# Tensors of the first stage stored by chunk, queries kept on chip, and new assumed durations in a planned two-layer decoder kernel

## The chip, the cores and the metric

The kernel runs on one core of one Trainium2 chip. The metric is the device time of one execution in microseconds (us), the median of three runs. The core has five engines with instruction streams of their own: TensorE (PE, matmuls and transposes), VectorE (DVE), ScalarE (ACT), GpSimd (POOL) and SyncE (SP), and DMA queues that are fed by SP, ACT and POOL.

## The reference

Two layers of a decoder for 2048 prompt tokens and 8 sample tokens, width 1024, fp32. Cut to what matters:

```
layer 0 (even):  p = rmsnorm(x) @ w_in -> val, gate, gate_a, q, k, v, z, beta, a
   A: c = conv31(val * sigmoid(gate)); silu(layernorm(c)) * silu(gate_a)
   B: q, k, v = silu(conv4(q, k, v)); gated delta rule over the tokens, 4 heads of 128:
        per chunk: u, w from a triangular solve of k, v, beta, decay
        v_new = u - w @ S;  o = q @ S + (q k^T * decay) @ v_new;  S = g * S + k^T @ v_new
      rmsnorm(o) * silu(z)
   x += concat(A, B) @ w_out
   x += cross_attention(rmsnorm(x), memory)           # 4 heads of 256, 256 memory rows
layer 1 (odd):   causal mean pooling over 2/4/8/16 tokens, a map per group, gate, w_out; then attention
y = rmsnorm(x);  also new conv, delta, pool states and memory keys and values
```

The sample tokens take the same path one step at a time, with cached memory keys and values of their own (8 x 256 rows for each layer).

## The kernel before

All activations lie transposed: channels on partitions, tokens on columns. A dense product is made of three fp32r matmuls (high x high, low x high, high x low), so each weight tile `rraw` is split into `rhi` and `rlo`, and each activation into a pair (`hh`/`hl`, `mh`/`ml`, `xh`/`xl`).

The stages: memory keys and values (`kv`, with the first norms beside it); the input projection in blocks of columns (gate, val, qkv, z) over five token tiles of 512, 512, 512, 260 and 260 columns, with the 31-tap convolution on DVE (`cacc`, 240 instructions over 1024 tokens each) and the 4-tap one (`qacc`); the delta rule over 16 chunks of 128 tokens, with matrices of the memory attention (`G`, `VW`, weights by memory) as dense filling; output projection; attention 0; the odd layer; attention 1 and the last norm. Beside these run the sample tokens' steps as side work.

The program has no hand-written order. A planner (class `Flow`, here `F`) writes it: every call (`F.mm`, `F.act`, `F.stt`, `F.dma` and so on) issues one instruction and moves an assumed clock of its engine by an assumed duration, and remembers at what assumed time each tile is written. Stages of dense matmuls are generators; after each piece `F.pump()` looks through the side tasks and runs one step of each whose inputs are ready by the assumed clock of PE. So the assumed durations set where the side work stands between the dense matmuls, and with that the order on every engine. `F.move`, `F.rows` and `F.ve` also choose ACT, DVE or POOL by these clocks. A DMA whose source isn't ready by the assumed clock is held back (`F.pend`) and issued later. The result is one fixed list of instructions for each engine; at run time each engine goes through its list in order and waits on semaphores.

Two assumed durations are touched. A matmul in fp32r of n columns costs `max(n, 248) * 0.422` ns. A DMA is assumed to start 650 ns after its issue, to move 360 bytes for each ns on one ring, and to be seen 900 ns later:

```
        x = max(g + 650, self.ring)
        self.ring = x + nb / 360.0
        self.mark(ri, ro, "dma", self.ring, self.ring + 900)
```

The assumed costs of DVE, ACT and POOL are not touched; that of a `cacc` (1024 columns by `F.stt`) is 1024/0.96 + 130 ns.

In the input projection, `fin_z` and the task after the 4-tap convolution store z and q, k, v to DRAM, `d_z` and `d_qkv`, in tiles `so` of 128 x 512, by head: `[4 or 12, 128, tokens]`. A bank `ps_mm` of a val block is free once DVE has written `glu` from it.

In the delta rule `prep(n)` loads k and q of a chunk, makes `qk` and `A`; later steps invert `A` by blocks (`ad`, `lo`, `UT`, `b`, `x`), `scan` walks the chunks with the state `S`, and a last task norms `o`, multiplies it with z and stores `d_b`. Q is loaded twice: by `prep` into `q` (three places), and by `scan` into `q2` (two places), two chunks ahead. In `scan`, PE runs `ps_bg<-S,k` and `ps_bg<-S,q2`, DVE makes `x`, PE `ps_bg<-x,A`, ACT or DVE `vn`, PE `ps_bg<-vn,kd` and `ps_bg<-vn,qk`, and DVE the new `S`.

Norms sum squares with a matmul of ones (`ps_ss`, from `acc` or `w_sqa`) and spread the result over partitions with a diagonal: DVE writes `dg` or `w_sqq<-ident,rr`, PE `ps_bc` (function `spread`; `tok_spread` calls it for the later stages). The sample's cross attention (`sample_attn`) loads cached keys and values through POOL's queue, 256 KB each, into three buffers `a_big`, with `d_sq` (the query spread out) or `d_sp` (the probabilities) in one of them for two loads of the cache, and DVE multiplies the two and sums: 128 products `a_big<-a_big` of 128 x 256 for each layer.

Of the kernel before, what the change touches and what calls it, by code (L numbers as in the profile page):

```python
# [55 lines left out]
class Flow:  # L56
# [106 lines left out]
    def mm(self, out, lhsT, rhs, start=True, stop=True, cost=None):  # L163
        n = fsz(rhs)
        if cost is None:
            cost = max(n, 248) * 0.422 if lhsT.dtype == F32R else max(n, 64) * 1.69
        self.pe_op(cost, out, lhsT, rhs)
        self.nc.tensor.matmul(out, lhsT, rhs, start=start, stop=stop)  # L168
# [123 lines left out]
    def _dma(self, out, in_, eng, t):  # L292
        ri, ro = [self.region(in_)], [self.region(out)]
        if eng == "sync" and out.space == DRAM and self.hand.get(in_.tensor.name) == {"act"}:
            eng = "scalar"
        s = max(self.t[eng], t, self.ready(ri, ro, eng))
        nb = 4
        for _, c in out.ap:
            nb *= c
        if eng == "scalar":  # L300
            s = max(s, self.t["act"])
            self.t["act"] = self.t[eng] = g = s + 360
        elif eng == "gpsimd":
            s = max(s, self.t["pool"])
            self.t["pool"] = self.t[eng] = g = s + 1060
        else:
            self.t[eng] = s + 50
            s = max(s, self.hw)
            self.hw = g = s + 475
        x = max(g + 650, self.ring)  # L310
        self.ring = x + nb / 360.0
        self.mark(ri, ro, "dma", self.ring, self.ring + 900)
        getattr(self.nc, eng).dma_start(out=out, in_=in_)
# [123 lines left out]
def spread(F, C, pool, ppool, r, n, tag, dg=None):  # L437

    ncn = (n + 127) // 128
    if dg is None:  # L440
        dg = pool.tile([128, ncn * 128], F32, tag=tag + "dg", name="dg")
    for c in range(ncn):
        F.ts(dg[:, c * 128:(c + 1) * 128], C.ident, r[:, c:c + 1], ALU.mult)
    yield
    ps = ppool.tile([128, 512], F32, tag="bg", name="ps_bc")
    F.mm(ps[:, 0:n], C.ones, dg[:, 0:n])
    return ps


def ceil128(n):  # L450
    return (n + 127) // 128 * 128
# [200 lines left out]
def phase1(F, C, I, D, st, P, R, mmp, bgp, loaders, mix, hp):  # L652
# [38 lines left out]
    with F.tile_pool(name="x1", bufs=1, side="right") as xp:  # L691
# [77 lines left out]
        def fin_z(b, t, n, ps):  # L769
            o = DT[t][0]  # L770
            z = sop.tile([128, 512], F32, tag="so", name="so", bufs=2)
            F.act(z[:, 0:n], ps[:, 0:n], AF.Silu)
            F.dma(D.z[b][:, o:o + n], z[:, 0:n])

# [147 lines left out]
    def conv4(b, t):  # L922
        yield qfree.ok
        qfree.take()
        r = rawt[b, t]
        acc = bp.tile([128, 512], F32, tag="qacc", name="qacc", bufs=2)
        F.copy(acc, r[:, 0:512], scale=C.scw[:, b, 0:1])
        for i in range(1, 4):
            F.stt(acc, r[:, i:i + 512], C.scw[:, b, i:i + 1], acc, ALU.mult, ALU.add)
        rfree.give()  # L930
        yield
        z = sop.tile([128, 512], F32, tag="so", name="so", bufs=2)
        F.act(z, acc, AF.Silu)
        F.dma(D.qkv[b][:, t * 512:(t + 1) * 512], z)
        qfree.give()
        qdone.add((b, t))
# [120 lines left out]
def phase2(F, C, I, D, st, P, fill, hp, mmp, bgp, after):  # L1057
# [15 lines left out]
    def small(tag, first, n, shape=(128, 4, 128)):  # L1073

        i = left[tag] = left.get(tag, -1) + 1
        return hp.tile(list(shape), F32, tag=f"h{first + i % n}", name=tag, bufs=1)

    hu = {}

    def room(tag, n):  # L1080

        q, b = (dx, 2) if n % 8 in (4, 5) else (cq, SL - 2)
        if tag == "A":
            return q.tile([128, 2, 4, 128], F32, tag=tag, name=tag, bufs=b // 2)
        return q.tile([128, 4, 128], F32, tag=tag, name=tag, bufs=b)
# [8 lines left out]
    gate = {n: getattr(st, n).rearrange("p (h c) -> p h c", h=4) for n in ("gc", "egc", "ekd", "gl")}  # L1094
    qkv = D.qkv.rearrange("(x h) p t -> x p h t", x=3)
    zv = D.z.rearrange("h p t -> p h t")

# [5 lines left out]
    def prep(n):  # L1103
        yield lambda: nxt[0] == n and cq and (n < 4 or dx) and slots.n >= 2 - n % 2 and (n < SL or n // 2 - (SL+1)//2 in done["T"])
        nxt[0] += 1
# [4 lines left out]
        X.A = X.A2[:, n % 2]  # L1110
        tok = slice(128 * n, 128 * n + 128)
        X.k = room("k", n)
        dec = small("dec", 0, NP)
        q = small("q", NP, NP)
        F.dma(X.k, qkv[1][:, :, tok])
        F.dma(q, qkv[0][:, :, tok])
        yield
# [37 lines left out]
        v = small("v", 2 * NP, 3)  # L1155
        F.dma(v, qkv[2][:, :, tok])
        F.now()
        ad = small("ad", 2 * NP + 3, NP, (128, 4, 48))
        a16 = ad[:, :, 32:48]
# [129 lines left out]

    def load_q(n):  # L1290
        q = big("q2", 2)
        F.dma(q, qkv[0][:, :, 128 * n:128 * n + 128])
        return q

    def scan():
        yield lambda: sq
        S = [sq.tile([128, 128], F32, name=f"S{h}") for h in range(4)]
        for h in range(4):
            F.memset(S[h], 0.0)
        qn = [load_q(0), load_q(1)]  # L1300
        for n in range(16):
            yield lambda: n in done["L"]
            X, q = hu[n], qn.pop(0)
            pk, pq = ps4(), ps4()
# [25 lines left out]
            F.tt(o, po, qs, ALU.add)  # L1330
            if n + 2 < 16:
                qn.append(load_q(n + 2))
                F.now()
            yield
# [7 lines left out]
    def onorms(i):  # L1342
        for n in range(i, 16, 2):
            yield lambda: n in oq
            o, ss = oq.pop(n)
            z = sq.tile([128, 4, 128], F32, tag=f"z{i}", name="z", bufs=1)
            F.dma(z, zv[:, :, 128 * n:128 * n + 128])
            F.now()
# [16 lines left out]
            F.stt(z, pt, C.dng[:, 0:1], z, ALU.mult, ALU.mult)  # L1365
            F.dma(D.b[n // 2].rearrange("h p t -> p h t")[:, :, 128 * (n % 2):128 * (n % 2) + 128], z)
            ofree.give()
# [118 lines left out]
def tok_spread(F, C, W, r, n):  # L1486
    return spread(F, C, W.p, W.bgp, r, n, "w", dg=W.t("sqq", [128, ceil128(n)]))

# [14 lines left out]
def e2(F, C, W, I, D, st, R, bdone, over, grow, spawn):  # L1503
# [33 lines left out]
    def prep():  # L1537
        for g in range(NG):
# [7 lines left out]
            b = W.t("f", [128, 4, n])  # L1546
            F.dma(b, D.b[g].rearrange("b p t -> p b t"))
            tb = F.cur
# [523 lines left out]
def sample_mix(F, C, p, bgp, I, D, st):  # L2072
# [144 lines left out]
    yield lambda: "z" in st.done  # L2217
    F.dma(zs, D.z.rearrange("h p t -> p h t")[:, :, SEQ:NT])
    F.tt(kd, o, o, ALU.mult)
# [5 lines left out]
    F.stt(o, o, C.dng[:, 0:1], zs.rearrange("p a b -> p (a b)"), ALU.mult, ALU.mult)  # L2225
    F.dma(D.b[0].rearrange("h p t -> p h t")[:, :, 256:264], o.rearrange("p (a b) -> p a b", a=4))
    yield lambda: free.n == 3
# [415 lines left out]
```

## Time and profile before

| | |
|---|---|
| median of three runs | 2902.09 us (2898.34 to 2905.38) |
| the profiled execution, its own time | 2902.86 us |
| its span | 2901.1 us |
| mean granted clock of PE | 0.972 |
| busy: PE / DVE / ACT / POOL | 2730.5 / 1968.4 / 1032.0 / 657.0 us |
| moved by DMA | 377.85 MB, 130 GB/s over the span |

The times are those of whole executions; the profile is one of them, and its span runs from the first to the last instruction that it shows. A row of a group names the line of the kernel, the engine, the operation, the tile written and the tiles read. Nearly all instructions are issued by helpers, so lines are those of helpers (L168 `mm`, L172 `tr`, L186 `act`, L219 `tt`, L225 `stt`, L232 `ts`, L313 a DMA) and the tiles tell what it is. A wait names the engine that stood, what it was about to do, and what it waited for last.

### The profile page before, as it was taken

To read this page: it belongs to the slowest core of one execution; us is meant where nothing else is said; L and a number is where in the kernel's file an instruction comes from. 1 tells how busy PE (TensorE), PEld (TensorE's weight loads), DVE (VectorE), ACT (ScalarE), POOL (GpSimd) and SP (SyncE) were. 2 spreads that over 40 slices of the span, in tenths; PEclk is the share of its full clock that TensorE was granted. 3 is DMA by queue.
4 is the path that set the end of the run, shared out by engine and by line. 5 is a ranking of instruction groups with operands and counts; after the bars stand their busy time and mean duration, and the time that the engine had idled before them with its cause. 6 is when DMAs were issued, how large, how long until landed. Compare 5 with 4: busy or idle time off the path is not lost.

```text
span 2901.1 us, 52440 instructions
## 1 busy us (share of the span) xinstructions
PE 2730.5 (94%) x20202; PEld 2498.5 (86%) x20202; DVE 1968.4 (68%) x4612; ACT 1032.0 (36%) x2448; POOL 657.0 (23%) x936
## 2 busy tenths in 40 slices
PE   7999999999998889799999999899999998999997
PEld 6878888888888778699898889899999997789987
DVE  6838999988667887776655556867755445765453
ACT  5632232233356455432321325443422122432321
POOL 3301112111054355122232320111011111221210
PEclk9999999999989899899999999999999999999998
DMA  7611122123455557565645434322545556422211
GB/s 240 213 48 41 46 75 65 46 77 113 129 148 160 154 165 230 172 228 183 211 149 169 144 117 140 116 70 74 173 134 165 181 165 206 136 78 68 70 59 52
DMA packets 269194, 377.85 MB, mean 130 GB/s; under 512 B 46096, under 2 KB 168208, under 8 KB 268944
## 3 DMA queue, kind: packets, MB, share of 16 engines
q1 hardware_dynamic: 211776, 264.77, 29.4%
q0 software_dynamic: 20864, 67.39, 7.5%
q10 hardware_dynamic: 36304, 42.34, 4.2%
q8 instruction: 159, 2.61, 0.4%
q14 instruction: 91, 0.75, 0.1%
HBM read 276.38 MB, written 96.40 MB: 128 GB/s over the span
## 4 chain that ended last, share of the span: by engine, by line
PE 34%; DMA 9%; DVE 6%; issue 2%; ACT 1%; POOL 1%; DVEq 0%; SPq 0%; POOLq 0%; ACTq 0%
PE ps_mm L168 32%; DMA a_big<-d_sp 2%; DVE a_big L225 1%; DMA a_big<-d_sq 1%; DMA a_big<-in_cache_v 1%; PE ps_pt L172 1%; DMA w_f<-d_x 1%; DVE rlo L225 1%; DVE w_d L219 1%; DMA rraw<-d_VW 1%; PE ps_row L168 1%; DVE rlo L219 1%; DVE ml L219 0%; DMA rraw<-d_G 0%; DMA a_big<-in_cache_k 0%
## 5 line engine op out<-in xcount | busy, mean ns | idle before, releaser
L219 POOL TENSOR_TENSOR rlo<-rraw,rhi 128x512 fp32r<-128x512 f32 x143 | 209.1, 1470 | 579.0 <-ACT rhi L186 495.5
L225 DVE SCALAR_TENSOR_TENSOR cacc<-glu,dww,cacc 128x1024 f32<-128x1024 f32 x240 | 325.6, 1369 | 5.9 <-ACT cacc L186 1.4
L219 POOL TENSOR_TENSOR w_sqb<-w_sqb,w_sqq 128x512 f32<-128x512 f32 (+1 forms) x101 | 137.1, 1357 | 660.9 <-ACT w_sqq L186 653.9
L168 PE MATMUL ps_mm<-xh,rhi 128*128 128x256 f32 (+1 forms) x1920 | 274.0, 285 | 5.3 <-DVE pool_sm L219 3.2
L168 PE MATMUL ps_mm<-xl,rhi 128*128 128x256 f32 (+1 forms) x1920 | 273.1, 284 | 0.0
L168 PE MATMUL ps_mm<-xh,rlo 128*128 128x256 f32 (+1 forms) x1920 | 272.7, 283 | 0.0
L168 PEld LDWEIGHTS ps_mm<-xh,rhi 128*128 128x128 f32 x1920 | 250.6, 192 | 8.6 <-issue 3.4
L168 PEld LDWEIGHTS ps_mm<-xl,rhi 128*128 128x128 f32 x1920 | 250.0, 192 | 2.6
L168 PEld LDWEIGHTS ps_mm<-xh,rlo 128*128 128x128 f32 x1920 | 248.2, 191 | 1.0
L168 PE MATMUL ps_mm<-hh,rhi 128*128 128x512 f32 (+2 forms) x1152 | 216.8, 329 | 20.2 <-ACT hh L186 15.8
L219 DVE TENSOR_TENSOR w_y<-ps_mm,w_y 128x256 f32<-128x256 f32 (+1 forms) x248 | 103.4, 420 | 165.6 <-PE ps_mm L168 161.2
L168 PE MATMUL ps_mm<-hh,rlo 128*128 128x512 f32 (+2 forms) x1152 | 214.6, 328 | 0.0
L168 PEld LDWEIGHTS ps_mm<-hh,rhi 128*128 128x128 f32 x1152 | 177.9, 191 | 42.0 <-ACT hh L186 16.2
L168 PE MATMUL ps_mm<-hl,rhi 128*128 128x512 f32 (+2 forms) x1152 | 211.7, 326 | 0.0
L225 DVE SCALAR_TENSOR_TENSOR a_big<-a_big 128x256 f32<-128x256 f32 x256 | 105.0, 448 | 144.5 <-DMA a_big<-d_sp 78.3
L186 ACT ACTIVATE rhi<-rraw 128x512 fp32r<-128x512 f32 x235 | 143.8, 628 | 164.0 <-DMA rraw<-d_G 41.5
L168 PEld LDWEIGHTS ps_mm<-hh,rlo 128*128 128x128 f32 x1152 | 175.9, 191 | 19.4 <-issue 2.2
L168 PEld LDWEIGHTS ps_mm<-hl,rhi 128*128 128x128 f32 x1152 | 175.4, 190 | 17.3
L168 PE MATMUL ps_mm<-mh,rhi 128*128 128x256 f32 (+1 forms) x1152 | 170.1, 288 | 11.8 <-ACT mh L186 11.7
L168 PE MATMUL ps_mm<-ml,rhi 128*128 128x256 f32 (+1 forms) x1152 | 170.5, 290 | 2.5 <-DVE ml L219 2.5
L168 PEld LDWEIGHTS ps_mm<-mh,rhi 128*128 128x128 f32 x1152 | 153.6, 195 | 14.5 <-ACT mh L186 12.8
L168 PE MATMUL ps_mm<-mh,rlo 128*128 128x256 f32 (+1 forms) x1152 | 165.6, 284 | 0.0
(425 smaller groups left out, 5344.5 us busy)
## 6 DMA issues: line engine op xcount, KB each, us to landing
w_f<-d_x SPq DMA_DIRECT2D x60, 512.0 KB
d_x<-w_y SPq DMA_DIRECT2D x44, 512.0 KB
w_y<-d_x SPq DMA_DIRECT2D x44, 512.0 KB
a_big<-in_cache_k POOLq DMA_DIRECT2D x64, 256.0 KB, 4.0
a_big<-in_cache_v POOLq DMA_DIRECT2D x64, 256.0 KB, 4.1
rraw<-in_w_in SPq DMA_DIRECT2D x56, 256.0 KB
d_qkv<-so ACTq DMA_DIRECT2D x48, 256.0 KB
rraw<-in_w_xk SPq DMA_DIRECT2D x32, 256.0 KB
```

The lines of the kernel that those rows point to most:

```text
L168: self.nc.tensor.matmul(out, lhsT, rhs, start=start, stop=stop)
L172: self.nc.tensor.transpose(out, in_, ident)
L186: self.nc.scalar.activation(out=out, in_=in_, func=func, scale=scale, **kw)
L219: self._e(eng).tensor_tensor(out=out, in0=a, in1=b, op=op)
L225: self._e(eng).scalar_tensor_tensor(out=out, in0=a, scalar=s, in1=b, op0=op0, op1=op1, **kw)
```

## The change

Three things are changed.

1. Assumed durations: an fp32r matmul of n columns now costs `max(n, 240) * 0.426 + 9` ns (512 columns: 227 for 216; 256: 118 for 108); a DMA starts 925 ns after its issue, moves 270 bytes for each ns, and is seen 1000 ns later.
2. Layouts: `d_qkv`, `d_z` and `d_b` are laid out by chunk, 128 partitions by 4 heads by 128 tokens, so that a load of a chunk takes 2 KB in one piece from each partition, and a store of 128 x 512 is written in pieces of 512 bytes. z of the sample tokens goes to a tensor of its own, and a tile of z that ends inside a chunk is stored in two pieces.
3. `q` of `prep` stays on chip until `scan` has read it, in one of eight places (`qplace`); `load_q` and its 16 loads go. `prep` waits, for two of eight chunks, until the pool `sq` of these places is open. `ad` has two buffers for three. And `spread` looks up the bank's pool after its yield instead of at the call.

```diff
-            cost = max(n, 248) * 0.422 if lhsT.dtype == F32R else max(n, 64) * 1.69
+            cost = max(n, 240) * 0.426 + 9 if lhsT.dtype == F32R else max(n, 64) * 1.69
...
-        x = max(g + 650, self.ring)
-        self.ring = x + nb / 360.0
-        self.mark(ri, ro, "dma", self.ring, self.ring + 900)
+        x = max(g + 925, self.ring)
+        self.ring = x + nb / 270.0
+        self.mark(ri, ro, "dma", self.ring, self.ring + 1000)
...
-    ps = ppool.tile([128, 512], F32, tag="bg", name="ps_bc")
+    ps = getattr(ppool, "bgp", ppool).tile([128, 512], F32, tag="bg", name="ps_bc")
...
-            F.dma(D.z[b][:, o:o + n], z[:, 0:n])
+            a = o
+            while a < min(o + n, SEQ):
...
+            if o + n > SEQ:
+                F.dma(D.zs[:, b, :], z[:, SEQ - o:NT - o])
...
-        F.dma(D.qkv[b][:, t * 512:(t + 1) * 512], z)
+        F.dma(D.qkv[b // 4, 4 * t:4 * t + 4, :, b % 4, :].rearrange("c p t -> p c t"), z.rearrange("p (c t) -> p c t", c=4))
...
+    def qplace(n):
+        i = n % 8
+        if i < 6:
+            return hp.tile([128, 4, 128], F32, tag=f"h{(NP, NP + 1, NP + 2, 11, 12, 13)[i]}", name="q", bufs=1)
+        return sq.tile([128, 4, 128], F32, tag="q", name="q", bufs=2)
...
-        yield lambda: nxt[0] == n and cq and (n < 4 or dx) and slots.n >= 2 - n % 2 and (n < SL or n // 2 - (SL+1)//2 in done["T"])
+        yield lambda: nxt[0] == n and cq and (n < 4 or dx) and (n % 8 < 6 or sq) and slots.n >= 2 - n % 2 and (n < SL or n // 2 - (SL+1)//2 in done["T"])
...
-        q = small("q", NP, NP)
-        F.dma(X.k, qkv[1][:, :, tok])
-        F.dma(q, qkv[0][:, :, tok])
+        q = X.q = qplace(n)
+        F.dma(X.k, D.qkv[1, n])
+        F.dma(q, D.qkv[0, n])
...
-        ad = small("ad", 2 * NP + 3, NP, (128, 4, 48))
+        ad = small("ad", 2 * NP + 3, 2, (128, 4, 48))
...
-    def load_q(n):
-        q = big("q2", 2)
-        F.dma(q, qkv[0][:, :, 128 * n:128 * n + 128])
-        return q
...
-            X, q = hu[n], qn.pop(0)
+            X = hu[n]
+            q = X.q
...
-            if n + 2 < 16:
-                qn.append(load_q(n + 2))
-                F.now()
...
-            F.dma(z, zv[:, :, 128 * n:128 * n + 128])
+            F.dma(z, D.z[n])
...
-        D.qkv = dr.tile([12, 128, SEQ], F32, name="d_qkv")
-        D.z = dr.tile([4, 128, NT], F32, name="d_z")
+        D.qkv = dr.tile([3, 16, 128, 4, 128], F32, name="d_qkv")
+        D.z = dr.tile([16, 128, 4, 128], F32, name="d_z")
+        D.zs = dr.tile([128, 4, 8], F32, name="d_zs")
...
-        D.b = [dr.tile([4, 128, gn(g)], F32, name=f"d_b{g}") for g in range(NG)]
+        D.b = [dr.tile([128, 4, gn(g)], F32, name=f"d_b{g}") for g in range(NG)]
```

The number of instructions of PE and POOL is the same before and after; by the order, DVE has 4383 for 4358, ACT 2310 for 2317, SP 969 for 982: some splits of weights (`rhi`, `rlo`, `gv`) have changed engine. How the order moves is shown at three places.

The first is DVE at the last block of val columns in the input projection, some 550 us into the program. `glu` is written once for each token tile and frees PE's bank; the `cacc` between are the 31-tap convolution of earlier columns. Before:

```order
L225 SCALAR_TENSOR_TENSOR qacc<-raw,scw,qacc 128x512 x3
L225 SCALAR_TENSOR_TENSOR cacc<-glu,dww,cacc 128x1024 x6
L225 SCALAR_TENSOR_TENSOR glu<-glu,ps_mm 128x512
L225 SCALAR_TENSOR_TENSOR cacc<-glu,dww,cacc 128x1024 x8
L225 SCALAR_TENSOR_TENSOR glu<-glu,ps_mm 128x512
L225 SCALAR_TENSOR_TENSOR cacc<-glu,dww,cacc 128x1024 x6
L225 SCALAR_TENSOR_TENSOR glu<-glu,ps_mm 128x512
L225 SCALAR_TENSOR_TENSOR cacc<-glu,dww,cacc 128x1024 x6
L225 SCALAR_TENSOR_TENSOR glu<-glu,ps_mm 128x260
L225 SCALAR_TENSOR_TENSOR cacc<-glu,dww,cacc 128x1024 x4
L225 SCALAR_TENSOR_TENSOR glu<-glu,ps_mm 128x252
```

And after, the same block:

```order
L225 SCALAR_TENSOR_TENSOR qacc<-raw,scw,qacc 128x512 x3
L225 SCALAR_TENSOR_TENSOR cacc<-glu,dww,cacc 128x1024 x6
L225 SCALAR_TENSOR_TENSOR glu<-glu,ps_mm 128x512
L225 SCALAR_TENSOR_TENSOR cacc<-glu,dww,cacc 128x1024 x6
L225 SCALAR_TENSOR_TENSOR glu<-glu,ps_mm 128x512
L225 SCALAR_TENSOR_TENSOR cacc<-glu,dww,cacc 128x1024 x10
L225 SCALAR_TENSOR_TENSOR glu<-glu,ps_mm 128x512
L225 SCALAR_TENSOR_TENSOR cacc<-glu,dww,cacc 128x1024 x4
L225 SCALAR_TENSOR_TENSOR glu<-glu,ps_mm 128x260
L225 SCALAR_TENSOR_TENSOR cacc<-glu,dww,cacc 128x1024 x4
L225 SCALAR_TENSOR_TENSOR glu<-glu,ps_mm 128x252
```

Here the same 24 `cacc` stand between the first and the last `glu`, spread otherwise; ahead of the first `glu` of this block stand 34 in place of 30 since the block before, and over the whole stage 182 of the 240 stand ahead of the last `glu` in place of 170.

The second is PE in the delta rule, between the third and the fourth step of the scan (some 900 us into the program; the numbers behind S are buffers). Before:

```order
L168 MATMUL ps_bg<-x,A 128x128 x4
L168 MATMUL ps_bg<-ident,gc 128x128 x4
L172 MATMUL ps_bg<-ident,k 128x128 x4
L168 MATMUL ps_bg<-vn,kd 128x128 x4
L168 MATMUL ps_bg<-vn,qk 128x128 x4
L168 MATMUL ps_bg<-S_7425,k 128x128
```

And after:

```order
L168 MATMUL ps_bg<-vn,kd 128x128 x4
L168 MATMUL ps_bg<-vn,qk 128x128 x4
L172 MATMUL ps_bg<-ident,dec 128x128 x4
L172 MATMUL ps_bg<-ident,q 128x128 x4
L168 MATMUL ps_mm<-rhi 128x512 x2
L168 MATMUL ps_mm<-rlo,rhi 128x512 x2
L168 MATMUL ps_mm<-rhi,rlo 128x512 x2
L172 MATMUL ps_bg<-ident,q 128x128 x4
L168 MATMUL ps_mm<-rhi 128x512 x2
L168 MATMUL ps_mm<-rlo,rhi 128x512 x2
L168 MATMUL ps_mm<-rhi,rlo 128x512 x2
L168 MATMUL ps_bg<-S_7438,k 128x128
```

Transposes of other chunks and twelve dense matmuls of `G` now stand between the last product that the new S needs and the first that reads it.

The third is DVE in the second sample attention, around the diagonal of a later token group (some 2346 us into the program); `a_oT` is where the sums of a product go. Before:

```order
L219 TENSOR_TENSOR w_d<-w_d,w_c 128x256
L219 TENSOR_TENSOR w_d<-ps_mm,w_rb 128x256
L219 TENSOR_TENSOR w_d<-w_d,w_c 128x256
L219 TENSOR_TENSOR ml<-w_d,mh 128x256
L225 SCALAR_TENSOR_TENSOR a_big,a_oT<-a_big 128x256 x2
L232 TENSOR_SCALAR w_sqq<-ident,rr 128x128 x2
L219 TENSOR_TENSOR ml<-w_d,mh 128x256
```

And after:

```order
L232 TENSOR_SCALAR a_mx<-a_mx 32x1
L242 RECIPROCAL a_sm<-a_sm 32x1
L232 TENSOR_SCALAR a_acc<-a_acc,a_sm 32x256
L219 TENSOR_TENSOR w_d<-w_d,w_c 128x256
L219 TENSOR_TENSOR ml<-w_d,mh 128x256
L232 TENSOR_SCALAR w_sqq<-ident,rr 128x128 x2
L219 TENSOR_TENSOR ml<-w_d,mh 128x256
```

At this diagonal the sample attention is now ten products behind where it was, and no product stands right ahead of it; at two other diagonals, where none did, one now does.

More of the change, by code (lines that the diff above doesn't have):

```diff
@@ L772, in fin_z @@
             F.act(z[:, 0:n], ps[:, 0:n], AF.Silu)
-            F.dma(D.z[b][:, o:o + n], z[:, 0:n])
+            a = o
+            while a < min(o + n, SEQ):
+                c, r = divmod(a, 128)
+                e = min(o + n, SEQ)
+                if r == 0 and e - a >= 128:
+                    k = (e - a) // 128
+                    F.dma(D.z[c:c + k, :, b, :].rearrange("c p t -> p c t"), z[:, a - o:a - o + 128 * k].rearrange("p (c t) -> p c t", c=k))
+                    a += 128 * k
+                else:
+                    k = min(128 - r, e - a)
+                    F.dma(D.z[c, :, b, r:r + k], z[:, a - o:a - o + k])
+                    a += k
+            if o + n > SEQ:
+                F.dma(D.zs[:, b, :], z[:, SEQ - o:NT - o])
         fin = {"z": fin_z}
@@ L1094, in phase2 @@
     gate = {n: getattr(st, n).rearrange("p (h c) -> p h c", h=4) for n in ("gc", "egc", "ekd", "gl")}
-    qkv = D.qkv.rearrange("(x h) p t -> x p h t", x=3)
-    zv = D.z.rearrange("h p t -> p h t")
     class HU:
@@ L1110, in prep @@
         X.A = X.A2[:, n % 2]
-        tok = slice(128 * n, 128 * n + 128)
         X.k = room("k", n)
         dec = small("dec", 0, NP)
-        q = small("q", NP, NP)
-        F.dma(X.k, qkv[1][:, :, tok])
-        F.dma(q, qkv[0][:, :, tok])
+        q = X.q = qplace(n)
+        F.dma(X.k, D.qkv[1, n])
+        F.dma(q, D.qkv[0, n])
         yield
@@ L1155, in prep @@
         v = small("v", 2 * NP, 3)
-        F.dma(v, qkv[2][:, :, tok])
+        F.dma(v, D.qkv[2, n])
         F.now()
-        ad = small("ad", 2 * NP + 3, NP, (128, 4, 48))
+        ad = small("ad", 2 * NP + 3, 2, (128, 4, 48))
         a16 = ad[:, :, 32:48]
@@ L1299, in scan @@
             F.memset(S[h], 0.0)
-        qn = [load_q(0), load_q(1)]
         for n in range(16):
             yield lambda: n in done["L"]
-            X, q = hu[n], qn.pop(0)
+            X = hu[n]
+            q = X.q
             pk, pq = ps4(), ps4()
@@ L1365, in onorms @@
             F.stt(z, pt, C.dng[:, 0:1], z, ALU.mult, ALU.mult)
-            F.dma(D.b[n // 2].rearrange("h p t -> p h t")[:, :, 128 * (n % 2):128 * (n % 2) + 128], z)
+            F.dma(D.b[n // 2][:, :, 128 * (n % 2):128 * (n % 2) + 128], z)
             ofree.give()
@@ L1486, in tok_spread @@
 def tok_spread(F, C, W, r, n):
-    return spread(F, C, W.p, W.bgp, r, n, "w", dg=W.t("sqq", [128, ceil128(n)]))
+    return spread(F, C, W.p, W, r, n, "w", dg=W.t("sqq", [128, ceil128(n)]))
 def mm3(F, R, W, name, j, x, n):
@@ L1546, in prep @@
             b = W.t("f", [128, 4, n])
-            F.dma(b, D.b[g].rearrange("b p t -> p b t"))
+            F.dma(b, D.b[g])
             tb = F.cur
@@ L2217, in sample_mix @@
     yield lambda: "z" in st.done
-    F.dma(zs, D.z.rearrange("h p t -> p h t")[:, :, SEQ:NT])
+    F.dma(zs, D.zs)
     F.tt(kd, o, o, ALU.mult)
@@ L2225, in sample_mix @@
     F.stt(o, o, C.dng[:, 0:1], zs.rearrange("p a b -> p (a b)"), ALU.mult, ALU.mult)
-    F.dma(D.b[0].rearrange("h p t -> p h t")[:, :, 256:264], o.rearrange("p (a b) -> p a b", a=4))
+    F.dma(D.b[0][:, :, 256:264], o.rearrange("p (a b) -> p a b", a=4))
     yield lambda: free.n == 3
```

## The prediction

> **What bounds the kernel now.** I read the busy times first, then a table by stage, then what TensorE (PE) waits for, and last the single waits with what stands around them. The page begins:
>
> ```profile
> span 2901.1 us, 52440 instructions
> PE 2730.5 (94%) x20202; PEld 2498.5 (86%) x20202; DVE 1968.4 (68%) x4612; ACT 1032.0 (36%) x2448; POOL 657.0 (23%) x936
> ```
>
> PE is the bound: it idles 171 us of 2901. The sum below is made against the profiled execution, 2902.86 us, which is 0.03% above the median of the three runs, 2902.09. The stages, by busy time of each engine and granted clock:
>
> ```profile
> 0.00:130.00 130.00, 105.79 (x807) 102.05 (x808) 100.75 (x161) 76.43 (x152) 49.99 (x51) 0.97 0.74 237
> 242.00:710.00 468.00, 457.09 (x2446) 396.33 (x2446) 435.58 (x457) 140.98 (x260) 76.81 (x57) 0.99 0.22 70
> 800.00:1215.00 415.00, 354.65 (x4147) 321.32 (x4146) 318.18 (x972) 231.87 (x756) 187.18 (x370) 0.90 0.58 168
> 1378.00:1670.00 292.00, 284.51 (x1830) 256.84 (x1829) 170.00 (x565) 81.08 (x176) 86.85 (x126) 0.99 0.53 167
> 2195.00:2475.00 280.00, 254.16 (x2027) 250.77 (x2026) 140.77 (x469) 58.25 (x118) 56.38 (x99) 0.95 0.57 181
> ```
>
> The columns are the stretch and its length, then busy PE, weight loads, DVE, ACT and POOL with counts, then clock, DMA share and GB/s. Two stages lose most: the delta rule (800 to 1215) idles PE 60 us and runs at 0.90, some 35 us more of slow matmuls (354.65 x 0.10); the second sample attention (2195 to 2475) idles 26 us and loses 13 to the clock. The convolutions (242 to 710) lose 11, but with DVE 93% busy. PE's waits over the whole span (engine, tile and line waited for; total, times, longest):
>
> ```profile
> PE ps_ss L168 <- POOL w_sqa L219: 16.1, 7, 5.0
> PE ps_bc L168 <- DVE w_sqq L232: 16.0, 9, 3.4
> PE ps_mm L168 <- ACT mh L186: 11.7, 4, 7.7
> PE ps_bg L168 <- DVE S L225: 11.3, 5, 4.3
> PE ps_bg L168 <- DVE lo L232: 9.7, 4, 4.3
> PE ps_mm L168 <- DVE glu L225: 8.1, 4, 3.8
> PE ps_bc L168 <- DVE dg L232: 5.5, 3, 3.3
> PE ps_cs L168 <- issue: 2.3, 1, 2.3
> PE ps_bg L172 <- DMA k<-d_qkv: 0.3, 1, 0.3
> ```
>
> PE nearly never waits for a load of the delta stage (the last row). What sets the time is the order in which side work lies between dense matmuls, and that order is what the new planner constants move.
>
> **The change part by part.**
>
> *Layouts, queries on chip, two `ad` buffers.* The 16 loads of `q2` (256 KB each, 4.2 MB) leave SP's queue, and z gains 12 stores on ACT's. No PE wait stands behind a q load, and that for k is 0.3 us, so I cost them 0. The bounds are -3 (what transfers hold back unseen elsewhere in that stage) and +5 (a step of the chain held until its query place is free; the nearest row is the longest wait for S, 4.3). The stores of q, k, v now go in 512-byte runs instead of 2 KB, and they lie where the DMA engines are 0.22 busy:
>
> ```profile
> L313 ACTq DMA_DIRECT2D d_qkv<-so x48: 326/326/362, 264.5 to 662.6; - x48
> ```
>
> Their first readers come a hundred microseconds later; 0, bounds 0 and +2.
>
> *Start.* The first broadcast of the norm (`ps_bc<-dg`) now follows the sums after 12 dense matmuls instead of 36. The pace of a matmul there:
>
> ```profile
> 30.59 1.10 PE L168 MATMUL ps_mm<-hh,rhi 128*128 128x256 f32 x8
> 31.53 1.11 PE L168 MATMUL ps_mm<-hl,rhi 128*128 128x256 f32 x8
> ```
>
> Eight start every 0.94 us, so the cover falls by 24 x 0.1175 = 2.8 us. The longest of the dg waits is 3.3 and grows by as much; the other two (2.2 together) change little: one broadcast gets more cover, one less. Sum +3, bounds 0 and +6.
>
> *Convolutions.* Here DVE sets the pace. Its only wait in this stage, and the group that fills it:
>
> ```profile
> DVE qacc L225 <- ACT qacc L186: 24.1, 28, 1.0
> L225 DVE SCALAR_TENSOR_TENSOR cacc<-glu,dww,cacc 128x1024 f32<-128x1024 f32 x240 | 325.6, 1369 | 5.9 <-ACT cacc L186 1.4
> ```
>
> Hops of 0.86 us each and nothing else: DVE never waits for PE. PE waits for it, at the end of each block of gate and value columns, since a bank is given back only when DVE has read it into `glu`:
>
> ```profile
> 322.97 3.80 DVE L225 SCALAR_TENSOR_TENSOR cacc<-glu,dww,cacc 128x1024 f32<-128x1024 f32 x3
> 326.69 0.68 DVE L225 SCALAR_TENSOR_TENSOR glu<-glu,ps_mm 128x512 f32<-128x512 f32 x1
> 327.43 1.22 PE L168 MATMUL ps_mm<-hh,rhi 128*128 128x260 f32 x8 [2.73 <-DVE glu L225]
> 561.35 2.20 PE L168 MATMUL ps_mm<-h,rhi 128*128 128x512 f32 x5 [3.78 <-DVE glu L225]
> ```
>
> The planner thinks matmuls slower than before, and leaves its price of a `cacc` as it was, so it finds room for more of them between two `glu`. Ahead of the last `glu` stand 182 of the 240 instead of 170. One `cacc` and the next start 1.36 us apart (325.6/240, nearly no gap): 12 x 1.36 = 16.3 us later for DVE, in steps of 2, 6 and 4 at three block ends. PE waits at each of these ends already, so it can't absorb any of it. After the last, PE runs on without DVE, so nothing is won back, except that the sample's first column sums come 11 us earlier in PE's order and the 2.3 us wait of `ps_cs` goes. Sum +14, bounds +8 (if a third of it was slack inside the blocks) and +18.
>
> The Trainium skill, TensorE: Matmul & The Clock Gate, section "Why this matters for your kernels", says to leave PE no gaps above some 3 us, since the clock then falls to half for a window. The trace agrees in the second sample attention (clock 0.95, gaps up to 7.7). By this rule the longer gaps here would cost half a window each; but with DVE as the bound that slowness is hidden at all ends but the last, and the sum would be +2 higher, within the bounds.
>
> *Delta rule.* The chain from step to step goes PE (vn,kd), DVE (S), PE (S,k):
>
> ```profile
> 904.92 1.11 DVE L225 SCALAR_TENSOR_TENSOR S<-S,gl,ps_bg 128x128 f32<-128x128 f32 x4
> 905.31 1.26 PE L168 MATMUL ps_bg<-S,k 128*128 128x128 f32 x8 [2.22 <-DVE S L225]
> ```
>
> I count the PE work that stands between vn,kd and the next S,k in the two orders, at such durations. In nine of the fifteen steps of before it is vn,qk alone (1.1 us); after, no cover but one (1.5) is under 2.4, and where PE waited for S it is 5.2, 5.6, 2.4, 11.5 and 4.3. These waits (11.3 in all) nearly go: -11. Of the waits for `lo` (9.7), two of four get 8 or more us more cover and the largest gets none: -4. The filling is finite: what covers these hops left other places (28.5 falls to 7.9, 19 to 3.9), and I take back 5 for hops that become bare, near the 4.3 of the longest wait. Sum -10, bounds -25 (with a clock of 0.94 instead of 0.90, worth 14) and +3.
>
> *End of the delta rule.* The first mean of the output norm comes 8 us later in PE's order and the last broadcast stands behind the last step's S,q, so that the first output matmul comes later by a hop. The nearest row is the longest wait there, 5.0 for `w_sqa`: +5, bounds 0 and +8. In the odd layer the cover of the sums falls from 5.9 to 4.5 us at four places that wait for POOL already: +2, bounds 0 and +5 (waits for `w_sqa`, 16.1 in seven).
>
> *Sample attention.* Its loads go through POOL's queue into three `a_big` buffers and DVE multiplies them, in order with the dense work:
>
> ```profile
> L225 DVE SCALAR_TENSOR_TENSOR a_big<-a_big x128: 414/421/955, 2195.5 to 2474.3; 128x256 f32<-128x256 f32 x128
> DMA a_big<-d_sp: 38.2, 13
> DMA a_big<-d_sq: 36.7, 13
> POOL a_big L313: 196.8, 57
> a_big<-d_sq POOLq DMA_DIRECT2D x32, 256.0 KB, 4.4
> a_big<-d_sp POOLq DMA_DIRECT2D x32, 256.0 KB, 4.4
> 2345.59 0.43 DVE L225 SCALAR_TENSOR_TENSOR a_big<-a_big 128x256 f32<-128x256 f32 x1 [2.50 <-DMA a_big<-d_sp]
> 2346.28 0.48 DVE L232 TENSOR_SCALAR w_sqq<-ident,rr 128x128 f32<-128x128 f32 x2
> 2346.82 1.17 PE L168 MATMUL ps_bc<-w_sqq,ones 128*128 128x256 f32 x2 [3.44 <-DVE w_sqq L232]
> ```
>
> The first rows say that DVE stood 75 us behind 26 late loads; the last three show how that reaches PE: the diagonal for the next broadcast stands behind the late product. A load lands 4.4 us after its issue. The planner reckoned 0.65 + 0.73 + 0.90 = 2.28 us for 256 KB and now reckons 0.93 + 0.97 + 1.00 = 2.90, so it puts a tile's product later among the dense matmuls. Between five successive `w_sqq` pairs stood 26, 24, 24 and 24 products; now 22, 20, 22 and 22: 14% more dense work for each. PE's full-pace work here is 280 - 38.5 = 241.5 us, 3.77 for each of 64 pairs of products, against 4.37 that passed (280/64); at 98/86 of 3.77 it becomes 4.30. If only the mean mattered, all but 4 us of the 38.5 would go: -34. But of the three buffers one holds a tile of d_sq or d_sp for two pairs, so that two loads in three are issued only when a pair is done, and the wait falls at every second pair. When I count PE's work between the first products of successive loads of d_sq or d_sp, and hold each such cycle to the 8.2 or so that it took where it waited,
>
> ```profile
> 2269.02 0.42 DVE L225 SCALAR_TENSOR_TENSOR a_big<-a_big 128x256 f32<-128x256 f32 x1 [5.24 <-DMA a_big<-d_sq]
> 2277.43 0.43 DVE L225 SCALAR_TENSOR_TENSOR a_big<-a_big 128x256 f32<-128x256 f32 x1 [4.06 <-DMA a_big<-d_sq]
> 2285.58 0.43 DVE L225 SCALAR_TENSOR_TENSOR a_big<-a_big 128x256 f32<-128x256 f32 x1 [2.98 <-DMA a_big<-d_sq]
> ```
>
> the loss falls only by about a third: -12; with cycles of 7.7 it falls by 4. Besides, at two of the four `w_sqq` a product now stands directly ahead where before none did. Bounds are -34 and -4; I take the middle, -20, since a shorter wait takes clock loss (13 of the 38.5) with it.
>
> The Trainium skill, DMA: Bandwidth & Descriptors, section "Anatomy of one DMA — SWDGE (gpsimd) path", gives 2.0 us and bytes over 436 GB/s, an estimate of 2.6 us here. The trace has 4.4 and decides; by the page's figure the new constants would already cover a load, and the gain would be the full -34.
>
> The first sample attention has the same waits on DVE but costs PE little (284.51 busy of 292, clock 0.99): -3, bounds -8 and +2.
>
> **Sum**: 3 + 14 - 10 + 5 + 2 - 20 - 3 = -9 us: 2894 against 2902.9.
>
> **The rivals.**
> - *The convolutions decide, slower.* Mechanism: 12 more `cacc` ahead of the last `glu` on a saturated DVE. For it: it follows from counts and a measured duration, while the gains follow from covers. Against: 38.5 us lie idle or slow in the second sample attention. Losses are 3 + 14 + 5 + 2 - 3 = 21; with the sample's gain at 5 and the delta stage's at 4, 2902.9 + 12 = 2915. It decides from the point where both gains together are under 15.
> - *Both stalls go.* The sample stage gains 34 and the delta stage 21, with its clock at 0.94: 2902.9 + 21 - 55 = 2869. For it: the mean rate now fits the loads. Against: the loads come in cycles of two pairs, and PE's filling in the delta stage has the same total.
> - *A wash.* The sample stage gains the 12 of the count by cycles, the delta stage 9: 2903. The planner's constants would then move stalls but not their sum.
> - *The change does not do what it says on chip*, since the queries were never late: that part holds in all cases here, and is costed at 0 already.
>
> **How the numbers follow.** About 0.2% (6 us) is what a measurement of this kernel can tell from no change. The forecast's case has a chance of 0.42, with a range of its own from 2883 to 2901; the convolutions 0.26; both stalls 0.14; the wash 0.18. Faster: most of the first and all of the third, 0.48. Slower: the second and a little of the wash, 0.27. Within: 0.25. The range from 2868 to 2917 reaches to the rivals on both sides and leaves out the ends where all bounds fall together.
>
> **What would show it.** In the profile after: waits of PE for `glu` near 8 + 16 us, and the 710 us point of before some 15 us later; waits for S under 3; in the second sample attention DVE's waits for d_sq and d_sp under 45 us and a clock of 0.97 or more. The forecast is wrong if `glu` waits stay at 8 (DVE had slack that I did not see), if S waits move to x or vn instead of going, or if PE's loss in the second sample attention stays above 30 us.

## Result and profile after

The changed kernel takes 2932.49 us (median of four runs, 2927.09 to 2933.84) against 2903.68: a ratio of 1.0099, 95% interval 1.008 to 1.0118. The forecast was 2894, with a range from 2868 to 2917. The profiled execution spans 2932.1 us, 31.0 more than before. Its busy times:

```profile
span 2932.1 us, 52475 instructions
PE 2733.7 (93%) x20202; PEld 2499.6 (85%) x20202; DVE 1990.5 (68%) x4637; ACT 1022.9 (35%) x2432; POOL 649.6 (22%) x936
```

PE does the same matmuls in the same busy time (3 us more); 28 of the 31 us are idle (2932.1 - 2733.7 against 2901.1 - 2730.5). DVE has 22 us more work, 13 of them splits of weights (`rhi`, `gv`) that ACT did before. To see where the time went I take, in each trace, the start of the same dense matmul (all traces hold 15,920 written to `ps_mm`, in nearly the same order) or of the first instruction of a stage, and list the time between these points:

| kernel | start | projection, convolutions | delta rule | attention 0, odd layer | second sample attention | rest |
|---|---|---|---|---|---|---|
| before | 235.2 | 540.5 | 424.7 | 986.4 | 315.9 | 398.4 |
| after | 241.5 | 565.0 | 436.6 | 987.5 | 299.4 | 402.1 |
| difference | +6.3 | +24.6 | +11.9 | +1.1 | -16.5 | +3.6 |

The delta rule counts from its first product (`ps_bg<-ident,gc`) to the first matmul of the output projection. The stages by the windows of the profile after, columns as before:

```profile
0.00:130.00 130.00, 102.48 (x769) 97.52 (x770) 99.25 (x161) 66.96 (x132) 55.90 (x53) 0.93 0.71 227
248.00:735.00 487.00, 459.03 (x2428) 397.08 (x2427) 453.17 (x483) 138.85 (x255) 70.24 (x54) 0.98 0.23 67
825.00:1255.00 430.00, 359.82 (x4192) 326.69 (x4190) 334.86 (x996) 239.41 (x776) 185.14 (x370) 0.88 0.53 159
2240.00:2506.00 266.00, 249.62 (x2036) 246.72 (x2036) 133.97 (x437) 58.21 (x118) 49.24 (x87) 0.98 0.57 181
```

PE idles 28 us in the convolutions (11 before) and 70 in the delta stage (60 before), whose clock is 0.88 instead of 0.90; in the second sample attention it idles 16 instead of 26 at a clock of 0.98 instead of 0.95. PE's waits over the whole span (rows that bear on what follows):

```profile
PE ps_ss L168 <- POOL w_sqa L219: 21.8, 9, 7.7
PE ps_bc L168 <- DVE w_sqq L232: 13.2, 11, 2.9
PE ps_mm L168 <- ACT raw L186: 10.4, 7, 3.5
PE ps_mm L168 <- DVE glu L225: 10.0, 4, 4.5
PE ps_bc L168 <- DVE dg L232: 8.3, 3, 4.0
PE ps_cs L168 <- issue: 7.6, 1, 7.6
PE ps_bg L168 <- DVE lo L232: 7.5, 3, 3.6
PE ps_bg L172 <- ACT o L186: 7.0, 2, 5.5
PE ps_mm L168 <- ACT mh L186: 6.6, 5, 1.9
PE ps_bg L172 <- DVE z L225: 4.6, 1, 4.6
PE ps_bg L168 <- DVE S L225: 4.0, 2, 3.5
```

Against the rows of before: the waits for S fell from 11.3 to 4.0 and those for `mh` from 11.7 to 6.6, as expected. Those for `glu` were to rise from 8.1 to some 24 and are 10.0. New are 10.4 us for `raw` (0.5 before), 4.6 for `z`, and 3.4 more for `o` of the delta rule; the wait of `ps_cs`, which was to vanish, grew from 2.3 to 7.6.

### The profile page after: what moved, and what is told of

Its sections match the earlier page's. It is cut to its first block, busy times and chain, and to the rows that moved or that the text cites. A ratio compares the mean times of both kernels' runs of the same rounds, so it can differ in the third digit from the quotient of the medians.

```text
span 2932.1 us, 52475 instructions
## 1 busy us (share of the span) xinstructions
PE 2733.7 (93%) x20202; PEld 2499.6 (85%) x20202; DVE 1990.5 (68%) x4637; ACT 1022.9 (35%) x2432; POOL 649.6 (22%) x936
## 4 chain that ended last, share of the span: by engine, by line
PE 41%; DVE 8%; DMA 8%; issue 2%; ACT 2%; POOL 1%; SPq 0%; DVEq 0%; ACTq 0%; POOLq 0%
PE ps_mm L168 37%; DMA a_big<-d_sq 2%; PE ps_bg L168 1%; DVE a_big L225 1%; PE ps_pt L172 1%; DMA w_f<-d_x 1%; PE ps_row L168 1%; DMA a_big<-d_sp 1%; DVE rlo L219 1%; DMA rraw<-d_VW 1%; POOL w_sqb L219 1%; DVE w_d L219 1%; PE ps_ss L168 1%; DMA rraw<-d_G 1%; PE ps_bc L168 1%
## 5 line engine op out<-in xcount | busy, mean ns | idle before, releaser
L186 ACT ACTIVATE rhi<-rraw 128x512 fp32r<-128x512 f32 x213 | 129.6, 627 | 139.6 <-DMA rraw<-d_G 31.7
```

Source lines behind the costliest of these rows:

```text
L186: self.nc.scalar.activation(out=out, in_=in_, func=func, scale=scale, **kw)
```

## Experiments

My theory: the matmul duration makes the loss in the convolutions, where DVE is the bound; the DMA durations make the gain in the second sample attention; layouts and queries on chip do little of themselves. Rivals: the 512-byte stores or the places of q cost the time; or the DMA durations make the convolutions late.

**The parts of the change apart.** Four kernels: e1 has the layouts and the queries on chip with both old durations; e2 is before with

```diff
-            cost = max(n, 248) * 0.422 if lhsT.dtype == F32R else max(n, 64) * 1.69
+            cost = max(n, 240) * 0.426 + 9 if lhsT.dtype == F32R else max(n, 64) * 1.69
```

e3 is the changed kernel without that line's change, and e4 is before with both new durations (the line above and the three of the DMA).

> Layouts by chunk and queries kept on chip alone, with the assumed durations of before. Theory (the new assumed durations move the time, the layouts do not): the order of the convolution stage and of the sample attention is that of before (170 cacc ahead of the last glu, 26, 24, 24, 24 products between diagonals), so 2898 to 2908 us in all, PE's position in the convolution stage within 3 us of before. Rival (the 512-byte stores and the new places for q cost the time): 2915 us or more, with PE 10 us or more late by the end of the convolutions.

> The kernel before with the new assumed matmul duration alone. Theory: 182 cacc stand ahead of the last glu as in the changed kernel, so the convolution stage loses the 25 us that the changed kernel loses there; the products of the second sample attention stand closer (30, 30, 26, 30 between diagonals), so that stage loses too, some 10 us: 2930 to 2945 us. Rival (the DMA durations or the layouts make the convolution stage late): within 8 us of before at the end of the convolutions.

> The changed kernel with the assumed matmul duration of before (layouts, queries and new DMA durations stay). Theory: the convolution stage is as before (170 cacc ahead of the last glu), the products of the second sample attention stand wider than in the changed kernel (20, 20, 20, 16 between diagonals), so it keeps that gain of 16 us or more: 2878 to 2895 us, faster than both kernels. Rival (the DMA durations cost the time in the convolution stage): 2915 us or more.

> Both new assumed durations, with the layouts and the second load of q of before. Theory: like the changed kernel in the convolution stage (182) and in the sample attention (22, 20, 22, 22), so within 8 us of the changed kernel's 2932. Rival (the layouts or the places for q cost the time): 2915 us or less, and the loss in the convolution or delta stage goes.

Measured, as ratios to before with their intervals, and differences to before by stage, in us:

| kernel | median us | ratio | start | convolutions | delta rule | att. 0, odd | second sample att. | rest |
|---|---|---|---|---|---|---|---|---|
| e1 layouts, q | 2901.23 | 0.999 (0.9969-1.0011) | +0.8 | -1.4 | -14.4 | +11.9 | -2.9 | +1.2 |
| e2 matmul | 2996.26 | 1.0315 (1.0281-1.035) | +6.5 | +25.2 | +7.8 | +52.7 | +8.2 | +2.3 |
| e3 layouts, q, DMA | 2907.67 | 1.0014 (1.0-1.0029) | +13.2 | -0.5 | +6.1 | +9.0 | -27.1 | +6.8 |
| e4 matmul, DMA | 2946.38 | 1.015 (1.012-1.0181) | +8.7 | +25.3 | +30.7 | -1.8 | -17.5 | +1.3 |
| after: all | 2932.49 | 1.0099 (1.008-1.0118) | +6.3 | +24.6 | +11.9 | +1.1 | -16.5 | +3.6 |

The convolutions are plain: +25 in the three kernels with the new matmul duration, nothing in the two without. So is the second sample attention: the fewer products stand between the diagonals, the shorter it is (30, 30, 26, 30: 324 us; 26, 24, 24, 24: 316; 22, 20, 22, 22: 299). In e3 the counts are 10, 20, 20, 16 in its trace, not 20, 20, 20, 16 as expected, since its sample attention begins between two diagonals: 289 us. Part of the gain is work that has only moved: of the 128 products all lie inside the stage in before, 10 behind its end in the changed kernel and 30 in e3. Stage and rest together are 12.8 us shorter in the changed kernel and 20.3 in e3. The window of the stage in e3 shows PE 281.92 busy of 289 us at a clock of 0.99; the second fence has DVE's waits there:

```profile
2215.00:2504.00 289.00, 281.92 (x2256) 275.66 (x2255) 155.24 (x467) 74.53 (x149) 51.38 (x88) 0.99 0.58 181
```

```profile
DVE a_big L225 <- DMA a_big<-d_sq: 29.7, 13, 3.9
DVE a_big L225 <- DMA a_big<-d_sp: 14.2, 9, 2.7
```

That is 44 us behind late loads, and 50 over all 128 products, instead of 75. Three expectations on whole times failed. e2 lost 93 us instead of some 25 to 40, since attention 0 lost 53. PE's waits for POOL's `w_sqa` are 37.2 us in attention 0 and the odd layer, 10.1 in before; that the sample's loads, which POOL issues too, stand too close there as well is likely, but not shown. e3 did not become the fastest kernel: its gain of 27 was given back at the start (13) and in the delta rule, attention 0 and the odd layer. e4 came 14 us above the changed kernel instead of within 8, where the delta rule alone took 18.8 more.

The delta rule was the surprise. Layouts and queries win there 14.4 us (before to e1) or 18.8 (e4 to after), the new DMA durations cost 20.5 (e1 to e3) or 22.9 (e2 to e4), and the new matmul duration 7.8 (before to e2) or 5.8 (e3 to after). As a whole the layouts and queries win nothing with the old durations (e1, ratio 0.999): attention 0 and the odd layer lose 11.9 us, as PE waits there 9.0 us for `xl` instead of 1.6, and 4.8 for an `o` of the delta rule behind the first output matmul, where before had no wait.

**DVE taken out of the convolutions.** In both kernels each `cacc` keeps its place and its assumed price but works on half of its columns; half of the 31-tap convolution is left out. Each ran once:

```diff
-            F.stt(acc, g[:, o + i:o + i + 1024], C.dww[:, b, i:i + 1], acc, ALU.mult, ALU.add)
+            F._op("dve", 1024 / 0.96 + 130, [acc], [g[:, o + i:o + i + 1024], C.dww[:, b, i:i + 1], acc])
+            F.nc.vector.scalar_tensor_tensor(out=acc[:, 0:512], in0=g[:, o + i:o + i + 512], scalar=C.dww[:, b, i:i + 1], in1=acc[:, 0:512], op0=ALU.mult, op1=ALU.add)
```

> The kernel before, every instruction in its place, but each cacc works on 512 of its 1024 columns (the rest of the 31-tap convolution is left out); the planner still reckons with 1024. Theory (DVE is the bound at the block ends of the convolution stage): the waits of PE for glu (8.1 us) and for the first sample sum (2.3) go, so PE leaves the stage (from 235 to 813 us of before) some 12 to 15 us earlier relative to its entry. Rival (PE is late there for another reason): no change beyond 3 us.

> The same halving of each cacc in the changed kernel (its order kept, half of the 31-tap convolution left out). Theory: glu, raw and first-sample-sum waits (10.0, 10.4 and 7.6 us) all go, and from entry to exit the convolution stage takes as long as in the halved kernel before, within 3 us: the 24 us between the two kernels in this stage vanish. Rival (the loss comes from PE's own order, or from the 512-byte stores): 10 us or more between the two halved kernels stay in this stage.

The stage took 525.3 us in the halved kernel before and 527.0 in the halved changed kernel: 24.6 us of difference shrink to 1.7. The window from 240 to 805 us, first the halved changed kernel, then the halved kernel before:

```profile
240.00:805.00 565.00, 564.00 (x3121) 490.24 (x3120) 375.77 (x679) 180.45 (x382) 69.59 (x88) 1.00 0.26 79
```

```profile
240.00:805.00 565.00, 564.92 (x3133) 491.52 (x3133) 374.24 (x681) 185.23 (x392) 77.50 (x101) 1.00 0.26 80
```

PE is 564 of 565 us busy in both, with the order of each kernel unchanged. That shows the cause: DVE's work stands in PE's way in this stage, in the kernel before as well (15 us). The delta stage of the halved changed kernel took 436.6 us all the same, so it isn't late because the convolutions are.

**Prices of the convolutions set to the traces**, in the changed kernel and that stage alone: 1360 ns for a `cacc` and 800 for a `qacc`, in the same form as above, at full width.

> The changed kernel with the planner's price of a cacc and a qacc set to what the traces show (1360 for 1197 ns, 800 for 663), in the convolution stage alone. 164 instead of 182 cacc then stand ahead of the last glu (170 in before), 104 instead of 124 ahead of the last of the block before. Theory (it is the ratio of the two assumed prices that puts too many cacc ahead of a glu): the stage's loss of 24 us goes and a few of the 11 us lost in before too, if the end of the convolutions doesn't become the bound; 2890 to 2910 us in all. Rival: 2922 us or more.

2895.43 us, ratio to before 0.9964 (0.9946 to 0.9981). `glu`, `raw` and `ps_cs` cost PE 1.5, 2.1 and 0.9 us:

```profile
PE ps_mm L168 <- ACT raw L186: 2.1, 1, 2.1
PE ps_mm L168 <- DVE glu L225: 1.5, 1, 1.5
PE ps_cs L168 <- DVE m_sq L219: 0.9, 1, 0.9
```

The border to the delta stage has moved in PE's order (4120 dense matmuls stand ahead of it instead of 4020), and 120 of the 576 matmuls of the filling stand ahead of the scan's first step instead of 66; so the two stages are taken together: from the start of the convolutions to the first output matmul 956.4 us, 1001.6 in the changed kernel, 965.2 in before.

**Old durations until the second sample attention**, new ones from there, with the layouts and queries on chip (a flag that `smp` sets):

> The new layouts with the assumed durations of before up to the start of the second sample attention, and the new ones from there. Theory: up to there as the layouts alone (2901 us in all), and 10 to 16 us less in the second sample attention (20, 20, 24 products between diagonals for 24, 24, 24): 2883 to 2893 us, faster than both kernels. Rival (the gain there needs the order of the whole changed kernel): 2898 us or more.

2892.17 us, ratio 0.995 (0.9932 to 0.9967); the second sample attention wins 14.1 us and the delta rule 12.0, attention 0 and the odd layer lose 8.7. So these gains can be had without the loss in the convolutions.

**Layouts and queries apart**, with the old durations.

> The kernel before with the queries kept on chip (second load gone, two ad buffers), its layouts and assumed durations unchanged. The dense filling stands between the steps of the scan as in the kernel with layouts and queries together (138 of 576 ahead of the fourth step, 282 ahead of the sixth), not as in before (132, 240). Theory (the 14 us that layouts and queries together win in the delta stage come from the new order, which the missing q2 loads make): 10 to 18 us less from the first step's products to the first output matmul (425 us in before). Rival (they come from the longer pieces of the loads): within 5 us of 425.

> The kernel before with the new layouts alone, q loaded twice, assumed durations of before. The filling stands as in before. Theory: the delta stage takes 425 us within 5, as in before; in all 2898 to 2908 us. Rival (the longer pieces of the loads bring the 14 us): 407 to 415 us in that stage.

Neither differs from before: 2903.62 us, ratio 0.9998 (0.9987 to 1.0009), and 2904.44, ratio 0.9998 (0.9986 to 1.0011). The delta stage took 5.2 us less with the queries on chip and 3.2 less with the layouts, against 14.4 for both in e1. The first expectation failed by half; how the 14 us divide stays open, since one trace for each kernel moves by some 5 us in that stage (before and e5, of the same order, differ by 4.8). The stage of the convolutions took 539.0 us with the new layouts: the 512-byte stores cost nothing.

**Filling held back.** The changed kernel, with the fp32r matmuls issued while `fill.run()` runs assumed 12% longer:

```diff
+        F.FX = 1.12
         F.run(fill.run())
+        F.FX = 1.0
```

> The changed kernel with the matmuls of the filling (G and VW, in the delta stage alone) assumed 12% longer than in the changed kernel, so that fewer stand at each hop: 372 of 576 ahead of the twelfth step (492 in the changed kernel, 426 in before), and 84 are left after the fifteenth (18, 60). Theory (the changed kernel spends its filling early and runs bare at the end, 58 us without filling before the first output matmul, 37 in before): the bare stretch shrinks under 45 us, waits for S come back, and the delta stage, 437 us in the changed kernel, takes 420 to 432. Rival (the stage loses by DVE's load or by other hops): 435 us or more.

2919.31 us, ratio 1.0056 (1.0035 to 1.0076), 13 less than the changed kernel. The delta stage took 417.7 us instead of 436.6. But the part of the theory on the bare end isn't borne out, nor did the waits for S come back (1.5 us). The time without filling ahead of the first output matmul shrank from 58 to 20 us, yet PE is as idle there as before. Over the 40 us that end 2 us behind the start of that matmul it is busy 18.90 and 17.33 us (changed kernel, then held filling):

```profile
1205.00:1245.00 40.00, 18.90 (x102) 16.01 (x101) 31.04 (x98) 19.85 (x58) 4.60 (x5) 0.67 0.44 136
```

```profile
1186.00:1226.00 40.00, 17.33 (x100) 14.45 (x99) 29.56 (x83) 17.45 (x42) 3.90 (x4) 0.78 0.67 205
```

60 fillers (matmuls of the filling) now lie behind the start of the last step instead of none. They are worth some 10 us: 36 have 256 columns at 0.117 us and 24 have 512 at 0.233. The time was won in the body, where that step starts 376 us after the stage's beginning instead of 410, which is 24 more than those fillers.

**All gains at once**: e8 with a `cacc` at 1270 and a `qacc` at 740 ns.

> New layouts and queries on chip, assumed durations of before until the second sample attention and the new ones from there, and a cacc and a qacc priced at 1270 and 740 ns in the convolution stage (162 cacc ahead of the last glu). Theory (the gains are of different stages and add): 2892 less some 8 to 15 us of the convolution stage: 2875 to 2886 us, faster than both kernels. Rival (the convolutions only end later, and the filling that moves ahead of the delta stage is missing there): 2890 us or more.

2898.58 us, ratio 0.9976 (0.9964 to 0.9989): not better than e8. The rival holds: from the convolutions' start to the first output matmul 961 us, against 953.9 in e8. PE waits 5 us in the convolutions instead of 10, but more of the filling stands ahead of the scan (168 fillers for 72), and its first step starts 27 us later than in e8 (886.5 for 859.0 us). DVE ends its last `cacc` 7 us later there, which is too little to be all of the reason; the rest stays open.

**The DMA durations in the delta stage alone** set back, everything ahead of it as in the changed kernel; and filling held back with the priced convolutions.

> The changed kernel with the DMA durations of before in the delta stage alone; all ahead of it as in the changed kernel. 408 of 576 fillers stand ahead of the twelfth step (492 in the changed kernel). Theory (the longer assumed loads and round trips through DRAM place each step later among the filling, which runs out before the scan's end): the stage takes 412 to 424 us instead of 437, all before it is as in the changed kernel within 3 us, and the whole 2908 to 2920 us. Rival (the stage is late because the convolutions end late, or by the matmul duration): 432 us or more.

> The changed kernel with the priced convolutions (1360 and 800 ns) and the filling held back (12% in the delta stage). Theory (the stage of the convolutions and the filling are two causes, but both spend the same spare work): from the start of the convolutions to the first output matmul 945 to 960 us (1002 in the changed kernel, 957 with priced convolutions, 983 with held filling), in all 2885 to 2897 us. If both added in full, 938 us and 2876; if they win the same time, 957 and 2895 or more.

e13: 2915.63 us, ratio 1.0035 (1.0022 to 1.0047); the delta stage took 418.2 us, 18.4 less than in the changed kernel, and the convolutions 565.9 as there. So here too the stage is not late because the convolutions are; the DMA durations in it cost it those 18 us. e14: 2890.53 us, ratio 0.9958 (0.994 to 0.9977), 954.7 us from the start of the convolutions to the first output matmul: held filling adds 2 us to the priced convolutions, not 19. What held filling wins alone is mostly the same time.

## Why the prediction was wrong

It failed by 38 us. Between the two profiles the sum is 40 us off: 12.5 in the delta rule, 10.6 in the convolutions, 4.4 at the end of the delta rule, 3.5 in the second sample attention, 3.3 at the start, 2.1 in attention 0 and the odd layer, and 3.6 in the rest, which had no term.

- *Convolutions, +14 predicted, +24.6 measured.* That DVE's lateness makes the loss was right (e5, e6), and so was its cause (e2, e7). The path to PE was only in part the predicted one: the sign for it, waits for `glu` near 24 us, failed. At the last `glu` PE was 10.5 us later than at the stage's entry (16.3 predicted), of which 1.9 are longer waits for `glu`, 5.0 waits for `raw`, and the rest slower matmuls. The step that made the term too small is "After the last, PE runs on without DVE, so nothing is won back": behind it PE lost 14 us more, at two places. First 7, 5.0 of them in waits for `raw`: `cacc` now also stand four in a row between two `qacc`. The place, in the changed kernel (the timelines of DVE, PE and ACT):

```profile
644.80 5.12 DVE L225 SCALAR_TENSOR_TENSOR cacc<-glu,dww,cacc 128x1024 f32<-128x1024 f32 x4
649.83 0.16 DVE L238 COPY raw<-raw 128x3 f32<-128x3 f32 x1
```

```profile
651.86 1.62 PE L168 MATMUL ps_mm<-h,rhi 128*128 128x512 f32 x4 [2.79 <-ACT raw L186]
```

```profile
650.09 0.72 ACT L186 ACTIVATE qacc<-raw,scw 128x512 f32<-128x512 f32 x1 [8.25 <-DVE raw L238]
651.23 0.58 ACT L186 ACTIVATE raw<-ps_mm 128x512 f32<-128x512 f32 x1
```

  DVE's small copy stands behind four `cacc`; ACT, in order, waits for it to start the next `qacc` and only then empties PE's bank into `raw`. The bank is tied to DVE here as at `glu`, by one engine more. The other place is the step "the 2.3 us wait of `ps_cs` goes". I moved it 11 us earlier in PE's order and did not ask when its input comes: `m_sq` stands behind 236 `cacc` on DVE, 224 in before. The wait grew (timelines of PE and of DVE, and the window around):

```profile
720.13 0.66 PE L168 MATMUL ps_cs<-m_sq,ones 128*128 128x64 f32 x2 [7.59 <-issue]
```

```profile
719.80 0.22 DVE L219 TENSOR_TENSOR m_sq<-m_s 128x64 f32<-128x64 f32 x1
```

```profile
715.00:740.00 25.00, 19.87 (x107) 17.24 (x108) 16.86 (x43) 6.32 (x9) 0.00 (x0) 0.86 0.30 98
```

  The mean clock of 0.86 around this gap agrees with the rule on gaps above 3 us that the prediction took from the Trainium skill (TensorE: Matmul & The Clock Gate, "Why this matters for your kernels").

- *Delta rule, -10 predicted, +2.5 measured; its end, +5 predicted, +9.4 measured.* Together they are the 11.9 of the table; the start of the last step's S,k parts them. The two parts, first before, then after:

```profile
775.67:1183.00 407.33, 358.73 (x4188) 324.55 (x4186) 309.05 (x963) 233.96 (x785) 184.29 (x368) 0.91 0.59 169
1183.00:1200.41 17.41, 8.48 (x52) 7.68 (x51) 14.12 (x33) 11.43 (x34) 2.88 (x2) 0.79 0.50 148
```

```profile
806.51:1216.35 409.84, 356.12 (x4181) 324.28 (x4180) 316.52 (x961) 234.84 (x790) 183.12 (x368) 0.90 0.52 156
1216.35:1243.16 26.81, 10.35 (x59) 7.78 (x57) 21.29 (x63) 13.87 (x38) 2.01 (x2) 0.68 0.34 107
```

  The step on S was right: its waits fell by 7.3 of the 11 foreseen, those for `lo` by 2.2 of 4. What failed is "I take back 5 for hops that become bare". PE idles 53.7 us in the body instead of 48.6, so some 15 us came back, in waits that before did not have: 4.6 each for `z` and for POOL's `w_sqa`, 3.5 more for `gv`, 3.1 for `bv`. At the end the term was too small and its reason wrong: the wait for `w_sqa` stayed (5.1 for 5.0), and new are 5.5 for `o` and 2.3 for `z`.

  The DMA durations made the loss: without them in that stage 18 us go (e13). How they make it stays open. In the changed kernel 492 of the 576 fillers stand ahead of the twelfth step, 426 in before and 408 in e13; but e4 has 408 too, and its stage is 23 us longer than that of e2, which has 444. The prediction read the 0.3 us that PE waited for a load of `k` for the layouts alone, and gave the longer assumed DMAs no price of their own in this stage. Nor does that row say that no transfer was late there: in before DVE, and PE behind it, did wait for one (timelines of DVE and of PE):

```profile
825.63 0.32 DVE L232 TENSOR_SCALAR lo<-UT,dn 128x128 f32<-128x128 f32 x1 [4.58 <-DMA UT<-x]
826.09 1.05 PE L168 MATMUL ps_bg<-lo,A 32*32 32x16 f32 x64 [4.29 <-DVE lo L232]
```

  For the layouts and queries, costed at 0, it was the wrong row as well: together they win 14 to 19 us in this stage.

- *Second sample attention, -20 predicted, -16.5 measured.* DVE still waited 75 us for d_sq and d_sp (45.8 and 29.0; under 45 was expected), so the loads came as late as before; PE felt it less, for `mh` 6.6 instead of 11.7 and at a clock of 0.98. The count by cycles alone (-12) and the middle (-20) lie on either side, and the middle was a choice; 10 products moved behind the stage's end as well. The measured 4.4 us landing was the right figure to judge by: with e3's wider order the gain was 27, so the 2.90 us that the planner now assumes seems still short.

- *Start, +3 predicted, +6.3 measured*: the waits for `dg` are 8.3 us instead of 5.5, the 2.8 foreseen, but the clock of the first 130 us is 0.93 instead of 0.97, which the term left out; PE's matmuls up to the stage's end took 2.3 us more.

- *First sample attention -3 and odd layer +2*: +1.1 measured together.

The first rival, that the convolutions decide, had the right cause and too low a price (2915): it left the delta stage a gain of 4, where there was a loss of 12.

## What to carry to other kernels

A planner's prices work by their ratio: correcting the matmul's alone, while DVE's stayed too low (1197 ns assumed, 1360 measured), cost 25 us in the stage that DVE bounds; correct the price of the bounding engine first, or both (e7). A wait that an edit moves must be priced from both ends: where the reader stands now, and when its input is ready now. Whether loads are late in a stage is not read from PE's waits alone: look at the engines that PE waits for. The same longer latencies won time in the second sample attention, where loads were late by 75 us, and cost 18 to 23 us in the delta stage, so try such constants stage by stage: the new ones from the second sample attention on made 2892.17 us.
